# Weight sums formed in place in the raw tiles of a hybrid-attention encoder layer, five raw blocks read instead of eight

## The chip, the cores and the metric

The kernel runs on one core of a Trainium2 chip. The metric is the device time of one execution in microseconds (us). A core has TensorE (PE, with its weight loads PEld), VectorE (DVE), ScalarE (ACT), GpSimd (POOL) and SyncE (SP); SP issues nearly all transfers here, each engine works through its own instructions in order, and engines wait for each other through semaphores.

## The reference

One encoder layer on 512 tokens of width 2048, in float32:

```python
h = rmsnorm(x, g_mix); proj = einsum('bsd,de->bse', h, w_in)      # 2048 -> 4608
out_a = rmsnorm(mixer_a(qa, ka, va, ...)); out_b = rmsnorm(mixer_b(qb, kb, vb))
x = x + einsum('bse,ed->bsd', concat([out_a, out_b]), w_out)
h2 = rmsnorm(x, g_ffn)
gate, up = split(einsum('bsd,df->bsf', h2, w_gate_up), 2)         # 2048 -> 2 x 5632
x = x + einsum('bsf,fd->bsd', silu(gate) * up, w_down)            # 5632 -> 2048
return rmsnorm(x, g_final)
```

## The kernel before, in words

The program has four stages in time: the input projection with the attention heads worked in between (0 to about 620 us), the output projection (`out_chunk`, kinds A and B, to about 732 us), eleven gate/up blocks (`gate_up_block`, to about 1630 us) and six down blocks (`down_block`, to about 2045 us), then a last plain piece of the down projection (`last_down`, `finish`).

Every float32 product is made of three PE matmuls in a reduced float32 type: each operand is split into a high part (an ACT copy) and a low part (a DVE subtraction), and `mm3` multiplies high by high, high by low and low by high. A 128x512 matmul takes one slot of the PE.

A gate/up or down block (`ColBlock`) is one two-by-two matrix product by seven products instead of eight (the forms m1, m7, m6, m2, m5, m4, m3, in this order, `CHAIN`). The activations' sums lie in the two `arena` tiles. The weights of a block come in quarters; for a batch g (there are four in a gate/up block and in the first four down blocks, two in the last two) the quarters are raw blocks of 128x1024, 512 KB each. Call them a = (0,0), b = (0,1), c = (1,1), d = (1,0). The seven forms need a; c-b; c-b+a; d; b-a; d-(c-b+a); c. One form of one batch is one unit (`Cols`): its weight operand is split into a "twin" tile tw (`split_hi` on ACT, L703; `split_lo` on DVE, L706), three twins exist (`TWINS`), and its matmuls are 12: two column pieces, two row tiles, three products. 28 units make a block of four batches.

Before the change each form loads its own raw blocks (tag raw, six buffers) and each sum is written to a tile of its own (tag sum, L732). a, b and c are loaded twice by this and, with d and m7's second operand, a batch reads eight blocks.

The order of the work is set by the program: for unit n, `prepare(n)` first issues loads (`load_raws`) as far as a look-ahead in time and the number of buffers allow, then makes the high part of a unit about 7 us ahead (`COLS_AHEAD`, two to three units), and the low part of the unit before that one; then come the matmuls of unit n, hooks (`box.after`) and one entry of the queue `side`. `load_raws` loads nothing further when the buffers are all held by blocks whose last unit has not had its low part made. Hooks of a gate/up block do the work on its results: `snap` copies a form's result out of PSUM, `low` and `high` multiply gate by up, `turn(k)` transposes 128 columns on the PE, `pair_sums` forms the sums of two turned pieces for the down blocks on DVE, and `store` writes them to DRAM. `h_side` does the same for the output projection's result: four transposes and an ACT copy for each half of a pair, then sums on DVE, a high part on ACT and a low part on DVE into `arena`. `ready` holds back the first block's matmuls on a pair until its `h_side` was issued.

Of the kernel before, what the change touches and what calls it, by code (L numbers as in the profile page):

```python
# [62 lines left out]
def encoder_block(ctx, tc, x, g_mix, w_in, g_q_a, g_k_a, g_out_a, g_out_b, w_out, g_ffn,  # L63
# [112 lines left out]

    def split(src, name, gain=None, between=None, at=None, tag=None):
        if at is None:
            hi, lo = (slot(name + "h", F32R), slot(name + "l", F32R)) if tag is None else (wslot(tag), wslot(tag))
# [23 lines left out]
    class Raw:  # L203
        def __init__(self, pieces, first=0):
            self.pieces, self.first, self.t = pieces, first, None

        def load(self):
            if self.t is None:
                self.t = wp.tile([P, 2 * 512], F32, tag="raw", bufs=RAWS, name=nm("raw"))
                for src, dst in self.pieces(self.t):  # L210
                    if self.first:
                        for a in range(src.shape[1]):
                            nc.sync.dma_start(dst[:, a], src[:, a])
                            load_x(self.first + a)
                    else:
                        nc.sync.dma_start(dst, src)
# [361 lines left out]
    def out_chunk(kind, c):  # L578
        box = {}
        base = 0 if kind == "A" else NHA  # L580

        def early(k):
            if (kind, k) not in oS:
                drain_until(lambda: (kind, k) in oT)
                oS[kind, k] = split(oT.pop((kind, k)), "oS", go[:, base + k:base + k + 1],
                                    at=42 + 2 * k if k < 7 else None, tag="wi")

# [12 lines left out]

        def mm(u, k):
            if k == 0:
                box["ps"] = [bank("pw") for _ in range(NT)]
# [4 lines left out]
            for t in range(NT):  # L608
                mm3(box["ps"][t], cols(oS[kind, k], t * P), u.w, k == 0, k == NHA - 1)

        def post():
# [9 lines left out]
            if kind == "B":  # L621
# [7 lines left out]
        add_chunk(w_out, [(base + k) * P for k in range(NHA)], [(c * 512, 0, 512)], mm, post,  # L629
                  early if kind == "B" else None,  # L630
# [9 lines left out]
    def pair_sums(w):  # L640
# [9 lines left out]
        tt(s4, b_l, s2)  # L650
        return w[:, 256:].rearrange("p (f c) -> p f c", c=256)

# [7 lines left out]
    def h_side(i, half):  # L660
        k = 2 * i + half
        c, j = divmod(k, 4)
        ps = bank("x1t")
        for n, t in enumerate((2, 3, 0, 1) if half == 0 else range(NT)):
            nc.tensor.transpose(ps[:, n * P:(n + 1) * P], x1[c][t][:, j * P:(j + 1) * P], ident)
        if half == 0:
            hpart[0] = sp.tile([P, 4 * 512], F32, tag="pair", bufs=1, name=nm("pair"))
        nc.scalar.activation(hpart[0][:, half * 512:(half + 1) * 512], ps, AF.Copy, scale=gf[:, k:k + 1])
# [23 lines left out]
    class Cols(Unit):  # L692
        ahead = COLS_AHEAD
        dur = COLS_US

# [4 lines left out]
        def split_hi(self):  # L700
            self.src = self.box.weights(self.form, self.g, *[r.t for r in self.raws])
            self.pair = sp.tile([P, 2, 2 * 512], F32R, tag="twin", bufs=TWINS, name=nm("tw"))
            nc.scalar.activation(self.pair[:, 0], self.src, AF.Copy)  # L703

        def split_lo(self):
            nc.vector.tensor_tensor(self.pair[:, 1], self.src, f32(self.pair[:, 0]), op=OP.subtract)  # L706

        def mm(self, u):
            self.box.multiply(self)

    class ColBlock:
        def __init__(self, w, row, lo, pairs, ready=None):
            self.pairs, self.ready = pairs, ready
            self.ps, self.sums = {}, {}
            self.begin = len(units)
            batches = pairs // 2

            def raw(i, j, g):
                def pieces(t):
                    rows = w[0, row + 4 * g * P:row + 4 * (g + 1) * P, lo[j]:lo[j] + 512]  # L720
                    return [(rows.rearrange("(q i p) c -> i p q c", q=2, i=2)[i],
                             t.rearrange("p (q c) -> p q c", q=2))]
                return Raw(pieces)
            need = {"m1": ((0, 0),), "m7": ((1, 1), (0, 1)), "m6": ((0, 0),), "m2": ((1, 0),),
                    "m5": ((0, 1), (0, 0)), "m4": (), "m3": ((1, 1),)}
            for form in CHAIN:
                for g in range(batches):
                    units.append(Cols(self, form, g, [raw(i, j, g) for i, j in need[form]]))

        def weights(self, form, g, *t):  # L730
            def tt(d, a, b, op=OP.subtract):
                nc.vector.tensor_tensor(d, a, b, op=op)  # L732
                return d

            def new():
                return sp.tile([P, 2 * 512], F32, tag="sum", bufs=SUMS, name=nm("sum"))
            if form == "m7":
                self.sums[g] = tt(new(), *t)
                return self.sums[g]
            if form == "m6":  # L740
                return tt(self.sums[g], self.sums[g], t[0], OP.add)
            if form == "m2":
                tt(self.sums[g], t[0], self.sums[g])
            if form == "m5":
                return tt(new(), *t)
            if form == "m4":
                return self.sums.pop(g)
            return t[0]

# [16 lines left out]
        def after(self, form, late, f):  # L766
            hook(self.begin + (CHAIN.index(form) + 1) * (self.pairs // 2) - 1 + late, f)

    def gate_up_block(f0):
# [50 lines left out]
        def store(n):  # L820
            nc.sync.dma_start(forms_dram[:, :, n], pair_sums(st["pair"]))

# [176 lines left out]
    def load_raws(n):  # L999
        while done["load"] < len(units) and at[done["load"]] <= at[n] + units[done["load"]].load_ahead:  # L1000
            for raw in units[done["load"]].raws:
                if raw.t is None:
                    live[:] = [r for r in live if last_use[r] >= done["lo"]]
                    if len(live) == RAWS:
                        return
# [108 lines left out]
```

## Time and profile before

| | |
|---|---|
| three runs | 2106.68, 2109.05, 2121.43 us; median 2109.05 |
| the profiled execution | 2104.86 us, span 2103.0 us, clock 0.99 |
| busy share of the span | PE 97%, PEld 79%, DVE 67%, ACT 47%, POOL 6% |
| moved | 419.78 MB, 200 GB/s in the mean |
| loads of gate/up weights | 352 of 512 KB |
| loads of down weights | 168 of 512 KB |
| chain that ended last | PE 72%, DMA 12%, DVE 10%, issue 3%, ACT 2% |

A row of a group gives line, engine, operation, output<-input and count, then busy time and the mean of one in ns, then the idle time of the engine just before these instructions and what ended it. A row of waits gives engine and instruction, what it waited for, total, times and longest in us.

### The profile page before, as it was taken

What the parts mean: (1) busy time and instruction counts of PE and PEld (TensorE: products, weight loads), DVE (VectorE), ACT (ScalarE), POOL (GpSimd) and SP (SyncE); (2) the same over time, 40 slices, a digit from 0 to 9 for tenths busy, and PEclk for the clock granted to TensorE, in tenths of its full rate; (3) what the DMA queues carried; (4) which work ended last, traced back from release to release, by engine and by line L of the source; (5) the groups of instructions that cost most, each with busy time, mean ns of one, the idle gap of its engine ahead of it and who ended that gap; (6) DMA issues with size and microseconds to landing.
All of it is one profiled execution on the core that took longest, in us unless ns stands there. A gap on an engine that the chain in (4) does not pass through costs nothing.

```text
span 2103.0 us, 24686 instructions
## 1 busy us (share of the span) xinstructions
PE 2037.1 (97%) x9159; PEld 1663.0 (79%) x9159; DVE 1418.2 (67%) x1862; ACT 985.5 (47%) x1406; POOL 129.6 (6%) x135
## 2 busy tenths in 40 slices
PE   9999999999999989999999999999999999999997
PEld 7888888888887768788888788888777777887876
DVE  5565655555645577777787777877778758757666
ACT  5333344444443544444444444444445455545663
POOL 3100100000000000000000000000000111111220
PEclk9999999999999999999999999999999999999999
DMA  7322222223343366677676676776778899999994
GB/s 232 104 80 81 86 71 81 81 76 106 120 166 122 101 213 215 226 252 230 228 253 228 220 242 225 243 236 232 242 240 278 262 264 328 295 247 327 266 316 172
DMA packets 238201, 419.78 MB, mean 200 GB/s; under 512 B 14800, under 2 KB 57856, under 8 KB 238080
## 3 DMA queue, kind: packets, MB, share of 16 engines
q1 hardware_dynamic: 224080, 392.96, 56.1%
q0 software_dynamic: 11808, 21.50, 6.0%
q10 hardware_dynamic: 2192, 3.74, 0.5%
q8 instruction: 71, 1.16, 0.2%
q14 instruction: 50, 0.41, 0.1%
HBM read 365.19 MB, written 52.95 MB: 199 GB/s over the span
## 4 chain that ended last, share of the span: by engine, by line
PE 72%; DMA 12%; DVE 10%; issue 3%; ACT 2%; SPq 1%; ACTq 0%; DVEq 0%; POOLq 0%
PE zc L195 8%; PE zc L196 7%; PE zc L194 7%; PE pj L194 6%; PE pj L196 6%; PE pj L195 6%; DMA raw<-in_w_down_dram 5%; DMA raw<-in_w_gate_up_dram 5%; PE yc L195 5%; PE yc L196 5%; PE yc L194 5%; DVE tw L706 4%; DVE sum L732 4%; PE pw L195 2%; PE pw L196 2%
## 5 line engine op out<-in xcount | busy, mean ns | idle before, releaser
L195 PE MATMUL zc<-tw,arena 128*128 128x512 f32 x1024 | 405.7, 396 | 28.8 <-DVE tw L706 28.7
L703 ACT ACTIVATE tw<-sum 128x1024 fp32r<-128x1024 f32 x256 | 269.5, 1061 | 323.0 <-DVE sum L732 205.3
L194 PE MATMUL zc<-tw,arena 128*128 128x512 f32 x1024 | 404.9, 395 | 3.5 <-ACT arena L672 2.8
L196 PE MATMUL zc<-tw,arena 128*128 128x512 f32 x1024 | 403.2, 394 | 1.3 <-DVE arena L673 1.3
L706 DVE TENSOR_TENSOR tw<-sum,tw 128x1024 fp32r<-128x1024 f32 x256 | 311.6, 1221 | 81.3 <-ACT tw L703 79.9
L706 DVE TENSOR_TENSOR tw<-raw,tw 128x1024 fp32r<-128x1024 f32 x192 | 234.7, 1223 | 125.5 <-ACT tw L703 123.8
L703 ACT ACTIVATE tw<-raw 128x1024 fp32r<-128x1024 f32 x192 | 203.1, 1059 | 205.5 <-PE zc L196 115.3
L195 PEld LDWEIGHTS zc<-tw,arena 128*128 128x128 f32 x1024 | 194.7, 190 | 78.7 <-DVE tw L706 39.0
L194 PE MATMUL pj<-w,arena 128*128 128x512 f32 x576 | 229.3, 398 | 1.2 <-ACT w L232 1.2
L194 PEld LDWEIGHTS zc<-tw,arena 128*128 128x128 f32 x1024 | 194.4, 190 | 44.4 <-ACT arena L672 3.2
L196 PEld LDWEIGHTS zc<-tw,arena 128*128 128x128 f32 x1024 | 194.9, 190 | 42.1 <-DVE arena L673 1.8
L195 PE MATMUL pj<-w,arena 128*128 128x512 f32 x576 | 225.3, 391 | 0.9 <-DVE w L237 0.9
L196 PE MATMUL pj<-w,arena 128*128 128x512 f32 x576 | 225.7, 392 | 0.0
L732 DVE TENSOR_TENSOR sum<-raw,raw 128x1024 f32<-128x1024 f32 x128 | 156.6, 1223 | 90.3 <-DMA raw<-in_w_down_dram 46.1
L195 PE MATMUL yc<-tw,arena 128*128 128x512 f32 x512 | 202.0, 395 | 10.7 <-DVE tw L706 10.7
L194 PE MATMUL yc<-tw,arena 128*128 128x512 f32 x512 | 202.9, 396 | 0.0
L196 PE MATMUL yc<-tw,arena 128*128 128x512 f32 x512 | 200.9, 392 | 0.0
L237 DVE TENSOR_TENSOR w<-raw,w 128x512 fp32r<-128x512 f32 x192 | 140.6, 747 | 27.2 <-ACT w L232 15.9
L890 POOL DMA_DIRECT2D x1d<-ev x82 | 72.4, 959 | 1238.7 <-ACT ev L889 1205.8
L232 ACT ACTIVATE w<-raw 128x512 fp32r<-128x512 f32 x192 | 115.1, 626 | 49.0 <-PE pj L196 25.9
L196 PEld LDWEIGHTS pj<-w,arena 128*128 128x128 f32 x576 | 108.5, 188 | 24.2 <-DVE arena L189 0.5
L195 PEld LDWEIGHTS pj<-w,arena 128*128 128x128 f32 x576 | 108.7, 189 | 23.5 <-DVE w L237 1.2
(201 smaller groups left out, 2995.6 us busy)
## 6 DMA issues: line engine op xcount, KB each, us to landing
raw<-in_w_gate_up_dram SPq DMA_DIRECT2D x352, 512.0 KB, 4.9
raw<-in_w_down_dram SPq DMA_DIRECT2D x168, 512.0 KB, 7.6
x1d<-ev POOLq DMA_DIRECT2D x82, 256.0 KB, 6.9
raw<-in_w_in_dram SPq DMA_DIRECT2D x38, 512.0 KB, 3.7
forms<-pair SPq DMA_DIRECT2D x20, 896.0 KB, 5.1
fr<-forms SPq DMA_DIRECT2D x35, 512.0 KB, 5.1
raw<-in_w_in_dram SPq DMA_DIRECT2D x68, 256.0 KB, 3.0
raw<-in_w_out_dram SPq DMA_DIRECT2D x32, 512.0 KB, 4.9
```

The costliest lines, as they stand in the source:

```text
L194: nc.tensor.matmul(dst, ah, bh, start=start, stop=False, skip_group_check=chained)
L195: nc.tensor.matmul(dst, ah, bl, start=False, stop=False, skip_group_check=chained)
L196: nc.tensor.matmul(dst, al, bh, start=False, stop=stop, skip_group_check=chained)
L232: nc.scalar.activation(self.w[0], src, AF.Copy)
L237: nc.vector.tensor_tensor(self.w[1], self.src, f32(self.w[0]), op=OP.subtract)
L703: nc.scalar.activation(self.pair[:, 0], self.src, AF.Copy)
L706: nc.vector.tensor_tensor(self.pair[:, 1], self.src, f32(self.pair[:, 0]), op=OP.subtract)
L732: nc.vector.tensor_tensor(d, a, b, op=op)
L890: nc.gpsimd.dma_start(x1_dram[2 * cb + j, row], e, accum_op=OP.add)
```

## The change

The raw blocks of a batch get a pool of their own (tag craw, ten buffers) and stay there; the sums are written over them. `fold`, a new function, runs right after the low part of the units m1 and m2. A batch now loads a and b (for m1), c (for m7), d (for m2), and c again as e (for m3). Loads for these units look 14 us ahead (`COLS_LOAD`) instead of 24 us. In the first block the unit m1 of batch 3 stands behind m7 of batches 0 and 1. `h_side` and the work on gate/up results are cut into more steps, with the store three units after the sums. The last chunk of the output projection takes its heads in the order 6, 7, 0 to 5, and its weight tiles are 12 instead of 10.

```diff
+COLS_LOAD = 14.0
-RAWS = 6
-SUMS = 6
-W_TILES = {"wi": 12, "wo": 10, "wl": 32}
+RAWS = {"raw": 6, "craw": 10}
+W_TILES = {"wi": 12, "wo": 12, "wl": 32}
...
+        order = [6, 7, 0, 1, 2, 3, 4, 5] if (kind, c) == ("B", NC - 1) else list(range(NHA))
...
                     side.append(lambda i=i: h_side(i, 1))
+                    side.append(lambda i=i: h_side(i, 2))
...
         if half == 1:
-            src = pair_sums(hpart.pop(0))
+            pair_sums(hpart[0])
+        if half == 2:
+            src = hpart.pop(0)[:, 256:].rearrange("p (f c) -> p f c", c=256)
             hi, lo = (arena[i // 4][:, :, i % 4, j] for j in range(2))
...
     class Cols(Unit):
         ahead = COLS_AHEAD
+        load_ahead = COLS_LOAD
...
         def split_lo(self):
             nc.vector.tensor_tensor(self.pair[:, 1], self.src, f32(self.pair[:, 0]), op=OP.subtract)
+            self.box.fold(self.form, self.g)
...
-            need = {"m1": ((0, 0),), "m7": ((1, 1), (0, 1)), "m6": ((0, 0),), "m2": ((1, 0),),
-                    "m5": ((0, 1), (0, 0)), "m4": (), "m3": ((1, 1),)}
+                return Raw(pieces, tag="craw")
+            self.raws = [{n: raw(i, j, g) for n, i, j in (("a", 0, 0), ("b", 0, 1), ("c", 1, 1), ("d", 1, 0),
+                                                          ("e", 1, 1))} for g in range(batches)]
+            need = {"m1": "ab", "m7": "cb", "m6": "ca", "m2": "dc", "m5": "a", "m4": "c", "m3": "e"}
+            order = [(form, g) for form in CHAIN for g in range(batches)]
+            if ready is not None:
+                order.insert(5, order.pop(3))
...
+        def weights(self, form, g):
+            t = {n: r.t for n, r in self.raws[g].items()}
             if form == "m7":
+                nc.vector.tensor_tensor(t["b"], t["c"], t["b"], op=OP.subtract)
             if form == "m6":
+                nc.vector.tensor_tensor(t["c"], t["c"], t["a"], op=OP.subtract)
+            return t[{"m1": "a", "m7": "b", "m6": "c", "m2": "d", "m5": "a", "m4": "c", "m3": "e"}[form]]
+
+        def fold(self, form, g):
+            t = {n: r.t for n, r in self.raws[g].items()}
+            if form == "m1":
+                nc.vector.tensor_tensor(t["a"], t["b"], t["a"], op=OP.subtract)
             if form == "m2":
+                nc.vector.tensor_tensor(t["c"], t["d"], t["c"], op=OP.subtract)
...
         for k in range(4):
-            box.after("m3", 4 + 2 * k, lambda k=k: turn(k))
+            late = (3, 4, 10, 11)[k]
+            box.after("m3", late, lambda k=k: turn(k))
             if k % 2 and f0 + k < F_PLAIN:
-                box.after("m3", 5 + 2 * k, lambda k=k: store((f0 + k) // 2))
+                box.after("m3", late + 1, lambda: pair_sums(st["pair"]))
+                box.after("m3", late + 4, lambda k=k: store((f0 + k) // 2))
```

How the instructions move is shown at two places, both at the form m7 of the fourth gate/up block. The first place is DVE. Before, where L706 is a low part, L732 a sum, L803 the product `high`:

```order
L706 TENSOR_TENSOR tw_8077<-raw_8003,tw_8077 128x1024 [waits DMAHW7_49,Activation_49]
L803 TENSOR_TENSOR s_1459_7692<-s_1459_7692,s_1469_7778 128x1024
L732 TENSOR_TENSOR sum_8116<-raw_8041,raw_8058 128x1024 [waits DMAHW2_49,DMAHW1_49]
L706 TENSOR_TENSOR tw_8098<-raw_8022,tw_8098 128x1024 [waits DMAHW0_49,Activation_49]
L732 TENSOR_TENSOR sum_8135<-raw_8075,raw_8096 128x1024 [waits DMAHW4_49,DMAHW3_49]
L706 TENSOR_TENSOR tw_8118<-sum_8116,tw_8118 128x1024 [waits Activation_49]
L732 TENSOR_TENSOR sum_8166<-raw_8114,raw_8133 128x1024 [waits DMAHW6_49,DMAHW5_49]
L706 TENSOR_TENSOR tw_8137<-sum_8135,tw_8137 128x1024 [waits Activation_49]
L732 TENSOR_TENSOR sum_8189<-raw_8162,raw_8164 128x1024 [waits DMAHW7_49,DMAHW0_49]
L706 TENSOR_TENSOR tw_8168<-sum_8166,tw_8168 128x1024 [waits PE_49,Activation_49]
```

DVE with the change, where L712 is a low part, L751 the fold of m1, L743 the sum of m7, L808 `high`, L649 the pair sums; raw_7888, 7907, 7928 and 7949 are b of batches 0 to 3, and raw_7966, 7984, 8072 and 8096 are c of batches 0 to 3:

```order
L712 TENSOR_TENSOR tw_7986<-raw_7926,tw_7986 128x1024 [waits DMAHW5_49,Activation_49]
L751 TENSOR_TENSOR raw_7926<-raw_7928,raw_7926 128x1024 [waits DMAHW6_49,DVE_49]
L808 TENSOR_TENSOR s_1406_7609<-s_1406_7609,s_1415_7694 128x1024
L743 TENSOR_TENSOR raw_7888<-raw_7966,raw_7888 128x1024 [waits DMAHW1_49]
L712 TENSOR_TENSOR tw_8006<-raw_7947,tw_8006 128x1024 [waits DMAHW7_49,Activation_49]
L751 TENSOR_TENSOR raw_7947<-raw_7949,raw_7947 128x1024 [waits DMAHW0_49,DVE_49]
L743 TENSOR_TENSOR raw_7907<-raw_7984,raw_7907 128x1024 [waits DMAHW2_49]
L712 TENSOR_TENSOR tw_8024<-raw_7888,tw_8024 128x1024 [waits Activation_49]
L743 TENSOR_TENSOR raw_7928<-raw_8072,raw_7928 128x1024 [waits DMAHW3_49]
L712 TENSOR_TENSOR tw_8048<-raw_7907,tw_8048 128x1024 [waits PE_49,Activation_49]
```

```order
L649 TENSOR_TENSOR pair_8045<-pair_8045 128x256 [waits DVE_49] x2
L743 TENSOR_TENSOR raw_7949<-raw_8096,raw_7949 128x1024 [waits DMAHW4_49]
L712 TENSOR_TENSOR tw_8075<-raw_7928,tw_8075 128x1024 [waits PE_49,Activation_49]
L745 TENSOR_TENSOR raw_7966<-raw_7966,raw_7886 128x1024
L712 TENSOR_TENSOR tw_8099<-raw_7949,tw_8099 128x1024 [waits Activation_49]
```

The second fence goes on where the first ends, less three rows of the pair sums. A fold now stands behind each low part of m1, and the sum of m7's batch 2, which waits for the transfer of c into raw_8072, stands right behind the low part that reads raw_7888 and ahead of the low part of batch 1.

The second place is SP, at the loads for the same units. Before:

```order
L216 DMA raw_8075<-in_w_gate_up_dram 128x2x512 [waits DMAHW5_49,DVE_49]
L216 DMA raw_8096<-in_w_gate_up_dram 128x2x512 [waits DMAHW6_49,DVE_49]
L216 DMA raw_8114<-in_w_gate_up_dram 128x2x512 [waits DMAHW7_49,DVE_49]
L216 DMA raw_8133<-in_w_gate_up_dram 128x2x512 [waits DMAHW1_49,DVE_49]
L216 DMA raw_8162<-in_w_gate_up_dram 128x2x512 [waits DMAHW2_49]
```

SP with the change:

```order
L216 DMA raw_7966<-in_w_gate_up_dram 128x2x512 [waits DMAHW1_49,DVE_49]
L216 DMA raw_7984<-in_w_gate_up_dram 128x2x512 [waits DMAHW2_49,DVE_49]
L216 DMA raw_8072<-in_w_gate_up_dram 128x2x512 [waits DMAHW3_49,DVE_49]
L216 DMA raw_8096<-in_w_gate_up_dram 128x2x512 [waits DMAHW4_49,DVE_49]
L216 DMA raw_8130<-in_w_gate_up_dram 128x2x512 [waits DMAHW6_49,DMAHW5_49,DVE_49]
L826 DMA forms<-pair_8045 896x1x256
```

The load into raw_8072 takes the buffer of raw_7888: with a and b of four batches and c of two, all ten buffers are held until the low part of m7's batch 0 (tw_8024) has read b of batch 0. The load into raw_8096 takes raw_7907's buffer in the same way, behind tw_8048. The store of the pair sums has no semaphore of DVE to wait for any more.

More of the change, by code (lines that the diff above doesn't have):

```diff
@@ L175, in rsqrt_mean, with split @@
         return r
-    def split(src, name, gain=None, between=None, at=None, tag=None):
+    def split(src, name, gain=None, between=None, at=None):
         if at is None:
-            hi, lo = (slot(name + "h", F32R), slot(name + "l", F32R)) if tag is None else (wslot(tag), wslot(tag))
+            hi, lo = slot(name + "h", F32R), slot(name + "l", F32R)
         else:
@@ L627, in post @@
                     side.append(lambda i=i: h_side(i, 1))
+                    side.append(lambda i=i: h_side(i, 2))
                 side.append(lambda: park_x1(c))
-        add_chunk(w_out, [(base + k) * P for k in range(NHA)], [(c * 512, 0, 512)], mm, post,
+        add_chunk(w_out, [(base + k) * P for k in order], [(c * 512, 0, 512)], mm, post,
                   early if kind == "B" else None,
@@ L660, in h_side @@
     def h_side(i, half):
[L661 to L668, printed above, removed]
+        if half < 2:
+            k = 2 * i + half
+            c, j = divmod(k, 4)
+            ps = bank("x1t")
+            for n, t in enumerate((2, 3, 0, 1) if half == 0 else range(NT)):
+                nc.tensor.transpose(ps[:, n * P:(n + 1) * P], x1[c][t][:, j * P:(j + 1) * P], ident)
+            if half == 0:
+                hpart[0] = sp.tile([P, 4 * 512], F32, tag="pair", bufs=1, name=nm("pair"))
+            nc.scalar.activation(hpart[0][:, half * 512:(half + 1) * 512], ps, AF.Copy, scale=gf[:, k:k + 1])
         if half == 1:
-            src = pair_sums(hpart.pop(0))
+            pair_sums(hpart[0])
+        if half == 2:
+            src = hpart.pop(0)[:, 256:].rearrange("p (f c) -> p f c", c=256)
             hi, lo = (arena[i // 4][:, :, i % 4, j] for j in range(2))
@@ L700, in split_hi @@
         def split_hi(self):
-            self.src = self.box.weights(self.form, self.g, *[r.t for r in self.raws])
+            self.src = self.box.weights(self.form, self.g)
             self.pair = sp.tile([P, 2, 2 * 512], F32R, tag="twin", bufs=TWINS, name=nm("tw"))
@@ L713, in __init__ @@
             self.pairs, self.ready = pairs, ready
-            self.ps, self.sums = {}, {}
-            self.begin = len(units)
+            self.ps, self.at = {}, {}
             batches = pairs // 2
@@ L722, in pieces @@
                              t.rearrange("p (q c) -> p q c", q=2))]
-                return Raw(pieces)
-            need = {"m1": ((0, 0),), "m7": ((1, 1), (0, 1)), "m6": ((0, 0),), "m2": ((1, 0),),
-                    "m5": ((0, 1), (0, 0)), "m4": (), "m3": ((1, 1),)}
[L726 to L736, printed above, removed]
+                return Raw(pieces, tag="craw")
@@ new lines, in __init__ @@
+            self.raws = [{n: raw(i, j, g) for n, i, j in (("a", 0, 0), ("b", 0, 1), ("c", 1, 1), ("d", 1, 0),
[4 more added lines that the diff above has]
+                order.insert(5, order.pop(3))
+            for form, g in order:
+                self.at[form] = len(units)
+                units.append(Cols(self, form, g, [self.raws[g][n] for n in need[form]]))
@@ L766, in after @@
         def after(self, form, late, f):
-            hook(self.begin + (CHAIN.index(form) + 1) * (self.pairs // 2) - 1 + late, f)
+            hook(self.at[form] + late, f)
     def gate_up_block(f0):
```

29 lines of the change are left out of this document (10 added, 19 removed).

## The prediction, made before the changed kernel ran

> **What bounds the kernel now.** I read the page's busy line first, then the waits of PE, then stretches of time, then one block's DVE rows.
>
> ```profile
> PE 2037.1 (97%) x9159; PEld 1663.0 (79%) x9159; DVE 1418.2 (67%) x1862; ACT 985.5 (47%) x1406; POOL 129.6 (6%) x135
> ...
> PE zc L195 <- DVE tw L706: 28.7, 22, 3.9
> PE yc L195 <- DVE tw L706: 10.7, 8, 4.0
> PE pw L195 <- DVE w L237: 5.3, 6, 1.6
> ```
>
> PE is the bound, and when it waits, it waits for DVE's low parts. So an edit counts only through what it does to these waits. How much is there to win? The stretches (columns: us, busy time and count of PE, PEld, DVE, ACT, POOL, then granted clock, DMA share, GB/s), two moments at which ACT copies m6 out of PSUM (in the first and the eleventh gate/up block), the first plain product after the down blocks, and two PE rows twelve matmuls apart with one group of four transposes:
>
> ```profile
> 660.00:760.00 100.00, 86.15 (x376) 67.64 (x375) 60.94 (x85) 49.12 (x75) 1.86 (x1) 0.95 0.40 128
> 779.00:1585.00 806.00, 792.17 (x3525) 648.27 (x3524) 608.86 (x614) 373.68 (x425) 0.00 (x0) 0.99 0.71 234
> 1585.00:2040.00 455.00, 433.57 (x1874) 352.03 (x1874) 322.18 (x280) 247.14 (x276) 70.62 (x80) 0.99 0.96 287
> ...
> 779.28 1.28 ACT L781 ACTIVATE s<-zc 128x512 f32<-128x512 f32 x2 [0.97 <-PE zc L196]
> 1584.58 1.28 ACT L781 ACTIVATE s<-zc 128x512 f32<-128x512 f32 x2 [1.34 <-PE zc L196]
> ...
> 2045.37 0.39 PE L194 MATMUL fd<-w,acth 128*128 128x512 f32 x1
> ...
> 1104.43 0.39 PE L195 MATMUL xc<-tw,arena 128*128 128x512 f32 x1
> 1107.15 0.39 PE L195 MATMUL zc<-tw,arena 128*128 128x512 f32 x1
> ...
> 834.33 0.44 PE at L810 x4
> ```
>
> A unit at full speed takes 1107.15 - 1104.43 = 2.72 us, so a gate/up block needs 28 x 2.72 + 4 x 0.44 = 77.9 us. From m6 of block 1 to m6 of block 11 are ten blocks: 1584.58 - 779.28 = 805.3 us against 779. About **26 us** are lost there in all, 2.6 a block. From there to the plain product are 16 + 140 units, 426 us with the transposes, and 460.8 pass: **35 us** lost. In the 100 us around the change from output projection to gate/up PE is idle for 13.9, and the clock of 0.95 costs some 5: **19 us**.
>
> One block's start on DVE (L706 low part, L732 sum, L800 `low`, L803 `high`):
>
> ```profile
> 1059.83 1.23 DVE L706 TENSOR_TENSOR tw<-raw,tw 128x1024 fp32r<-128x1024 f32 x1 [1.45 <-ACT tw L703]
> 1060.97 1.28 DVE L800 TENSOR_TENSOR s<-zc,s 128x512 f32<-128x512 f32 x2
> 1062.55 1.23 DVE L706 TENSOR_TENSOR tw<-raw,tw 128x1024 fp32r<-128x1024 f32 x1 [0.30 <-ACT tw L703]
> 1063.69 1.22 DVE L803 TENSOR_TENSOR s<-s,s 128x1024 f32<-128x1024 f32 x1
> 1064.82 1.22 DVE L732 TENSOR_TENSOR sum<-raw,raw 128x1024 f32<-128x1024 f32 x1
> 1065.96 1.22 DVE L706 TENSOR_TENSOR tw<-raw,tw 128x1024 fp32r<-128x1024 f32 x1
> 1067.09 1.22 DVE L732 TENSOR_TENSOR sum<-raw,raw 128x1024 f32<-128x1024 f32 x1
> 1068.31 1.22 DVE L706 TENSOR_TENSOR tw<-sum,tw 128x1024 fp32r<-128x1024 f32 x1
> 1070.42 1.23 DVE L732 TENSOR_TENSOR sum<-raw,raw 128x1024 f32<-128x1024 f32 x1 [0.89 <-DMA raw<-in_w_gate_up_dram]
> 1071.57 1.22 DVE L706 TENSOR_TENSOR tw<-sum,tw 128x1024 fp32r<-128x1024 f32 x1
> 1073.78 1.22 DVE L732 TENSOR_TENSOR sum<-raw,raw 128x1024 f32<-128x1024 f32 x1 [0.99 <-DMA raw<-in_w_gate_up_dram]
> ```
>
> Three things are to be seen: back to back such an instruction costs 1.135 us (1064.82 to 1065.96); `low` begins when the block before has ended, so the block starts near 1060.8, call it T; and a late transfer stops DVE for about 1 us only, because each load is issued three or more DVE instructions ahead of its use.
>
> **The change, part by part.** *Transfers.* A batch reads five blocks instead of eight, so 520 loads of 512 KB become 325. DVE's work does not fall: four sums a batch before, four now (m7, m6 and the two folds). PE's and ACT's work is the same. So nothing is won but waits.
>
> *The new wait.* The order on DVE puts the sum of m7's batch 2 right behind the low part that frees the buffer its transfer needs. SP cannot issue that load earlier, DVE has nothing else to do until it lands, and the low part of m7's batch 1, for which PE waits next, is queued behind. Batch 3 repeats it, with only the pair sums (1.56 us in the trace) for cover. Its price comes from these rows (two windows, and the raw tiles from 1050 to 1080 us):
>
> ```profile
> raw<-in_w_gate_up_dram SPq DMA_DIRECT2D x4, 512.0 KB, 3.6
> raw<-in_w_gate_up_dram SPq DMA_DIRECT2D x9, 512.0 KB, 6.0
> L216 SPq DMA_DIRECT2D raw<-in_w_gate_up_dram x13: 367/368/462, 1050.2 to 1075.0; - x13
> L703 ACT ACTIVATE tw<-raw x6: 1061/1062/1062, 1050.6 to 1064.2; 128x1024 fp32r<-128x1024 f32 x6
> DMA to landing us min/median/max: 3.5/3.9/7.6
> ```
>
> With few loads in flight (1115 to 1135 us) a block lands in 3.6 us, among many (1060 to 1080) in 6.0. At the new place hardly another load is in flight, so I take 3.6, plus 0.37 of issue and an estimated 0.1 for signals: 4.1. Then:
>
> - From `low` to the low part of m7's batch 0 DVE has `low` (1.28) and eight instructions of 1.135, 10.4 us, pushed back by up to 1.1 by the fold ahead of `low`: done at T + 10.6 to 11.7.
> - PE starts m7's batch 0 at T + 4 x 2.72 + 2 x 0.44 = T + 11.8, just served. It wants the low part of batch 1 one unit and one matmul later, T + 14.7.
> - That low part comes after 4.1 + 1.2 (sum) + 1.2: T + 17.1 to 18.2. PE stands for 2.4 to 3.5 us.
> - The low part of batch 2 comes another 6.5 later, T + 23.6 to 24.7, and would have been wanted at T + 17.4. So the block is 6.2 to 7.3 us late, **7 taken**.
> - After that DVE needs 2.27 a unit against PE's 2.72 and gets ahead again. The late loads of d (m2, batches 2 and 3) have about two to four us of DVE work between buffer and use and come just in time by the same count, since PE has two transposes there: nothing.
>
> Bounds for this: below, DVE could be as far ahead as the three twins allow. The twin for m7's batch 0 comes free when m1's batch 1 ends, T + 5.4, then 1.06 on ACT and 1.23 on DVE: T + 7.9. Then the second wait ends at T + 21 and the block is 3.6 late. Above, with 6.0 to land, both waits grow by 2.4, to 12.
>
> Ten blocks (2 to 11) have this: 10 x 7 = 70, and the 26 lost there now goes, because each other load has ten or more us of DVE work ahead of it. **+44 us** (bounds +10 and +94).
>
> *Down blocks.* Here DVE has no `low`, `high` or pair sums, so the low part of m7's batch 0 ends near T + 9.5, but transfers share the queues with accumulations, at a DMA share of 0.96 before. I take 5.0 to land. Blocks one and three have both waits, as on the gate/up side: 9.5 + 2 x (5.5 + 2.4) = 25.3 against 16.5, 9 late each; blocks two and four have one, with copies of the sums into `arena` between: about 6 each (estimate, between one wait's 3.6 and 9); the last two, of two batches, fit in ten buffers, 4 together. That is 34 against 35: **0** (bounds -25, if the lighter traffic frees the stage, and +20, at the stage's old landing:
>
> ```profile
> raw<-in_w_down_dram SPq DMA_DIRECT2D x166, 512.0 KB, 7.6
> SPq L821 <- DVE pair L646: 115.8, 20, 6.5
> ```
>
> first row). The second row is what SP waited at the store of the pair sums. That wait goes, but the loads behind it are held by their buffers now, so I give it nothing; were they not, it would be worth up to 6 us of SP's time a store.
>
> *Start of gate/up.* `h_side` in three steps keeps DVE from standing behind ACT's copy into `arena`, and the moved m1 gives the last pairs two units more. Of the 19 us I take **-12** (bounds 0 and -19). The new order of the last chunk and two more weight tiles belong to this.
>
> *Sum.* The profiled execution took 2104.9: 2104.9 + 44 + 0 - 12 = 2136.9. The median of the runs is 4.2 above it, so the forecast on that scale is **2141 us**.
>
> A rule to weigh: PE's clock. The row that bears on it is a wait of PE in the eleventh block, from the chain of waits:
>
> ```profile
> 1511.90 1.23 DVE sum L732
> 1513.13 1.15 DVE tw L706
> 1514.32 0.67 PE zc L195
> 1514.99 0.43 PE zc L196
> ...
> 1518.23 0.23 PE zc L195
> ```
>
> After it matmuls come at 0.43 instead of 0.23 us for about nine of them, 1.8 us. In my sum this is free: slower matmuls after the first wait only shorten the second, which ends on DVE. The Trainium skill, "TensorE: Matmul & The Clock Gate", Part 1, says the clock halves after an idle window of about 3.4 us that runs freely, so a gap near that length sometimes escapes. My first gap lies at that length.
>
> **The rivals.**
>
> 1. *Half clock after the second wait, or slower landing.* If the first gap leaves the clock alone, the second is 6.5 - 2.5 = 4 us long and 1.8 follow, ten times: 2159. With landing at 6.0: 2141 + 50 = 2191. For it: the row of 6.0. Against: a lone load.
> 2. *DVE is far enough ahead.* The lower bound of 3.6 a block: 2141 - 34 = 2107, no change. For it: in the rows above DVE still waits for ACT at the start of the block. Against: from there to m7 it is busy without a gap, with three folds more.
> 3. *Faster: the traffic was the price.* The down stage runs at a share of 0.96, and a batch now needs five blocks of eight. If lighter queues clear the stage (-25), the start gives all its 19, and the lower bound holds: 2109 + 10 - 25 - 19 = 2075. It decides from the point where landing in the down stage falls below about 4 us. Against it: two waits a block that no traffic makes.
> 4. *It does not act.* The order shows it does; 2109 if some other wait ends last in each block.
>
> **How the numbers follow.** A measurement of this kernel can tell about 1%, 21 us. Forecast 0.48, rival 1 0.20, rival 2 0.16, rival 3 0.13, rival 4 0.03. Slower by over 1% (above 2130): rival 1 and most of the forecast, 0.63. Within 1%: rivals 2 and 4 and the lower edge of the forecast, 0.23. Faster by over 1%: 0.14. The forecast's own range is 2120 to 2165; the range of eight in ten reaches from 2086, which leaves out most of rival 3, to 2188.
>
> **What would show it.** Right: in each of blocks 2 to 11 the sum of m7 waits for the transfer of gate/up weights twice, about 4 and 2.5 us; PE waits for DVE tw twice a block, 65 to 75 us in all; a block lasts about 85 us; the DMA share falls from 0.71 to about 0.45 in gate/up; the stretch at 660 to 760 is about 12 us shorter. Wrong: blocks of 80 us or less, or DVE that waits there without PE waiting; or a down stage that changes by more than 20 us.

## The result and the profile after

The changed kernel takes 2179.21 us (median; 2177.59 to 2183.56) against 2107.97 us for the kernel before on the same chip: a ratio of 1.0326, interval 1.0281 to 1.0371. Slower was forecast, with gate/up as the place; the size was not, nor any loss in the down stage: 32 us forecast, 71 measured. The profiled execution took 2180.45 us with a span of 2178.3, 75.3 us more span than before.

The busy line of the changed kernel:

```profile
PE 2061.0 (95%) x9159; PEld 1676.4 (77%) x9159; DVE 1420.7 (65%) x1862; ACT 989.8 (45%) x1406; POOL 129.9 (6%) x135
```

DVE's work is what it was (1418.2 before). Its waits and PE's (L712 is now the low part, L743 the sum of m7; total, times, longest in us):

```profile
PE yc L195 <- DVE tw L712: 72.9, 30, 5.4
DVE raw L743 <- DMA raw<-in_w_gate_up_dram: 61.5, 20, 3.8
DVE raw L743 <- DMA raw<-in_w_down_dram: 27.4, 6, 6.1
PE zc L195 <- DVE tw L712: 9.7, 8, 1.8
```

and, of the first of these rows, the part in the ten blocks from 772 to 1636 us:

```profile
PE yc L195 <- DVE tw L712: 51.4, 20, 3.9
```

PE's wait at yc, the bank of m7 (and of m4), was 10.7 us in the whole kernel before, only 0.4 of it in these ten blocks. Now it is 72.9, and 51.4 of it stand here. DVE's twenty waits in gate/up are two in each of ten blocks. The stretches, with the columns of those before:

```profile
660.00:760.00 100.00, 88.98 (x408) 70.45 (x407) 70.28 (x93) 51.41 (x77) 1.86 (x1) 1.00 0.38 128
772.00:1636.00 864.00, 811.83 (x3521) 659.78 (x3520) 610.61 (x615) 378.58 (x425) 0.00 (x0) 0.97 0.48 146
1636.00:2119.00 483.00, 444.26 (x1890) 357.75 (x1889) 324.80 (x284) 251.03 (x286) 72.36 (x82) 0.98 0.77 206
```

ACT's copy of m6 in blocks 1 and 11 and the first plain product, in the order of time:

```profile
771.73 1.28 ACT L786 ACTIVATE s<-zc 128x512 f32<-128x512 f32 x2 [0.98 <-PE zc L196]
1635.87 1.28 ACT L786 ACTIVATE s<-zc 128x512 f32<-128x512 f32 x2 [0.54 <-PE zc L196]
2119.28 0.39 PE L194 MATMUL fd<-w,acth 128*128 128x512 f32 x1
```

So m6 of block 1 comes 7.5 us earlier, the ten blocks from there take 864.1 us instead of 805.3 (**+58.8**), the down stage 483.4 instead of 460.8 (**+22.6**), the tail 1.4 more. The DMA share in gate/up fell from 0.71 to 0.48 and the time rose.

The first part of m7 in one block on DVE (L649 pair sums):

```profile
1087.05 1.22 DVE L712 TENSOR_TENSOR tw<-raw,tw 128x1024 fp32r<-128x1024 f32 x1
1091.95 1.23 DVE L743 TENSOR_TENSOR raw<-raw,raw 128x1024 f32<-128x1024 f32 x1 [3.69 <-DMA raw<-in_w_gate_up_dram]
1093.10 1.22 DVE L712 TENSOR_TENSOR tw<-raw,tw 128x1024 fp32r<-128x1024 f32 x1
1094.23 1.54 DVE L649 TENSOR_TENSOR pair<-pair 128x256 f32<-128x256 f32 x4
1098.19 1.22 DVE L743 TENSOR_TENSOR raw<-raw,raw 128x1024 f32<-128x1024 f32 x1 [2.42 <-DMA raw<-in_w_gate_up_dram]
1099.34 1.22 DVE L712 TENSOR_TENSOR tw<-raw,tw 128x1024 fp32r<-128x1024 f32 x1
```

The low part ends, its buffer is free, DVE stands 3.7 us for the transfer into it, makes the sum and only then the low part that PE wants; then once more, with the pair sums as cover. And PE in two later blocks (each row a matmul, L195 the one that reads the low part; in the brackets PE's idle time):

```profile
1176.40 0.39 PE L194 MATMUL yc<-tw,arena 128*128 128x512 f32 x1
1179.63 0.50 PE L195 MATMUL yc<-tw,arena 128*128 128x512 f32 x1 [2.85 <-DVE tw L712]
...
1182.30 0.39 PE L194 MATMUL yc<-tw,arena 128*128 128x512 f32 x1
1185.74 0.79 PE L195 MATMUL yc<-tw,arena 128*128 128x512 f32 x1 [3.05 <-DVE tw L712]
1186.33 0.63 PE L196 MATMUL yc<-tw,arena 128*128 128x512 f32 x1
1186.76 0.63 PE L194 MATMUL yc<-tw,arena 128*128 128x512 f32 x1
...
1441.02 0.79 PE L195 MATMUL yc<-tw,arena 128*128 128x512 f32 x1 [2.69 <-DVE tw L712]
1441.61 0.63 PE L196 MATMUL yc<-tw,arena 128*128 128x512 f32 x1
...
1445.06 0.40 PE L194 MATMUL yc<-tw,arena 128*128 128x512 f32 x1
1447.05 0.50 PE L195 MATMUL yc<-tw,arena 128*128 128x512 f32 x1 [1.59 <-DVE tw L712]
```

In the first of them the matmuls behind the second gap come 0.43 us apart (1186.33 to 1186.76) instead of 0.23: half clock. In the second the half clock lies between the two gaps, and the second gap is so much shorter. Such blocks differ in length by 3 us (from m6 to m6; granted clock in the third column from the right):

```profile
1291.26:1378.99 87.73, 81.84 (x353) 66.47 (x352) 60.80 (x62) 37.49 (x43) 0.00 (x0) 0.96 0.46 141
1378.99:1463.78 84.79, 80.44 (x353) 65.47 (x352) 60.63 (x62) 37.50 (x43) 0.00 (x0) 0.98 0.48 146
```

### The profile page after: what moved, and what is told of

Same layout as the page of the kernel before. It is cut to its first block, busy times and chain, and to the rows that moved or that the text cites. A ratio compares the mean times of both kernels' runs of the same rounds, so it can differ in the third digit from the quotient of the medians.

```text
span 2178.3 us, 24416 instructions
## 1 busy us (share of the span) xinstructions
PE 2061.0 (95%) x9159; PEld 1676.4 (77%) x9159; DVE 1420.7 (65%) x1862; ACT 989.8 (45%) x1406; POOL 129.9 (6%) x135
## 4 chain that ended last, share of the span: by engine, by line
PE 38%; DVE 10%; DMA 9%; issue 6%; ACT 2%; POOL 1%; SPq 0%; ACTq 0%; POOLq 0%; DVEq 0%
PE zc L196 6%; PE zc L194 6%; PE zc L195 6%; DVE tw L712 5%; DMA raw<-in_w_gate_up_dram 4%; PE yc L195 4%; PE yc L196 4%; PE yc L194 4%; DMA raw<-in_w_down_dram 3%; DVE raw L743 2%; PE xc L195 2%; ACT tw L709 1%; PE xc L196 1%; PE xc L194 1%; POOL x1d L897 1%
## 5 line engine op out<-in xcount | busy, mean ns | idle before, releaser
L709 ACT ACTIVATE tw<-raw 128x1024 fp32r<-128x1024 f32 x448 | 471.3, 1059 | 599.7 <-PE zc L196 181.0
L712 DVE TENSOR_TENSOR tw<-raw,tw 128x1024 fp32r<-128x1024 f32 x448 | 545.3, 1222 | 293.6 <-ACT tw L709 283.0
L195 PE MATMUL zc<-tw,arena 128*128 128x512 f32 x1024 | 400.5, 391 | 9.7 <-DVE tw L712 9.7
L195 PE MATMUL yc<-tw,arena 128*128 128x512 f32 x512 | 214.6, 419 | 72.9 <-DVE tw L712 72.9
L195 PEld LDWEIGHTS zc<-tw,arena 128*128 128x128 f32 x1024 | 192.9, 188 | 51.6 <-DVE tw L712 12.6
L195 PE MATMUL pj<-w,arena 128*128 128x512 f32 x576 | 225.1, 391 | 0.9 <-DVE w L237 0.9
L194 PE MATMUL yc<-tw,arena 128*128 128x512 f32 x512 | 211.3, 413 | 0.6 <-ACT tw L709 0.6
L196 PE MATMUL yc<-tw,arena 128*128 128x512 f32 x512 | 210.6, 411 | 0.0
L195 PEld LDWEIGHTS yc<-tw,arena 128*128 128x128 f32 x512 | 102.8, 201 | 108.0 <-DVE tw L712 86.6
L743 DVE TENSOR_TENSOR raw<-raw,raw 128x1024 f32<-128x1024 f32 x64 | 78.1, 1221 | 89.0 <-DMA raw<-in_w_gate_up_dram 61.5
L196 PEld LDWEIGHTS pj<-w,arena 128*128 128x128 f32 x576 | 108.4, 188 | 23.7
L195 PEld LDWEIGHTS pj<-w,arena 128*128 128x128 f32 x576 | 108.6, 189 | 23.4 <-DVE w L237 1.2
L194 PEld LDWEIGHTS pj<-w,arena 128*128 128x128 f32 x576 | 108.5, 188 | 23.4 <-ACT w L232 1.1
```

The source lines that it names most:

```text
L194: nc.tensor.matmul(dst, ah, bh, start=start, stop=False, skip_group_check=chained)
L195: nc.tensor.matmul(dst, ah, bl, start=False, stop=False, skip_group_check=chained)
L196: nc.tensor.matmul(dst, al, bh, start=False, stop=stop, skip_group_check=chained)
L743: nc.vector.tensor_tensor(t["b"], t["c"], t["b"], op=OP.subtract)
```

## The experiments

All times by stage, each from one profiled execution (m6 of block 1; the ten blocks from there to m6 of block 11; from there to the first plain product), with the median of the runs and the ratio to the kernel before:

| kernel | m6 at | ten blocks | down | median | ratio, interval |
|---|---|---|---|---|---|
| before | 779.3 | 805.3 | 460.8 | 2107.97 | |
| after | 771.7 | 864.1 | 483.4 | 2179.21 | 1.0326, 1.0281 to 1.0371 |
| e1 two c | 772.1 | 785.6 | 450.6 | 2068.32 | 0.9810, 0.9781 to 0.9840 |
| e2 low parts first | 780.0 | 856.7 | 506.0 | 2200.19 | 1.0437, 1.0403 to 1.0472 |
| e3 swap everywhere | 772.2 | 820.0 | 477.1 | 2129.90 | 1.0099, 1.0067 to 1.0130 |
| e4 forms on POOL | 772.7 | 861.2 | 489.6 | 2185.05 | 1.0364, 1.0326 to 1.0402 |
| e5 one wait | 769.8 | 825.9 | 470.5 | 2129.19 | 1.0110, 1.0067 to 1.0154 |
| e6 weave | 771.8 | 785.5 | 469.9 | 2086.64 | 0.9894, 0.9857 to 0.9930 |
| e7 old turns, stores | 770.4 | 872.6 | 496.7 | 2203.17 | 1.0462, 1.0423 to 1.0500 |
| e8 start alone | 770.7 | 804.6 | 468.0 | 2101.66 | 0.9969, 0.9947 to 0.9992 |
| e9 weave, forms on POOL | 769.9 | 785.1 | 477.1 | 2093.45 | 0.9921, 0.9899 to 0.9942 |
| e10 two c, forms on POOL | 774.6 | 785.7 | 447.2 | 2067.91 | 0.9798, 0.9777 to 0.9818 |
| e11 weave before | 769.1 | 807.7 | 465.1 | 2100.10 | 0.9948, 0.9929 to 0.9968 |
| e12 weave, two d | 771.5 | 784.7 | 457.8 | 2073.16 | 0.9825, 0.9798 to 0.9852 |

**e1: is the transfer of c the price?**

```diff
+            for g in range(2, batches):
+                self.raws[g]["c"] = self.raws[g - 2]["c"]
             need = {"m1": "ab", "m7": "cb", ...
```

> Leaves out: batches 2 and 3 of a gate/up or down block take their c from the tiles of batches 0 and 1, so two of the 20 loads of a four-batch block are not made (m7, m6, m2 and m4 of these batches multiply wrong weights); every instruction on PE, DVE and ACT stays. Theory (the late transfer of c in m7 is the price): DVE no longer waits at the sum of m7, a gate/up block falls from 86.4 to about 78.5 us, ten blocks give back 75 to 80, the four large down blocks another 10 to 20: about 2085 us (2070 to 2100). Rival (DVE's own work, four sums and folds in new places, is what is late): PE goes on waiting for DVE tw about 80 us and the time stays within 15 us of 2179.

Its busy line, and from the order of time ACT's copies of m6 in blocks 1 and 11 (the code stands two lines lower in this kernel):

```profile
PE 2023.3 (98%) x9159; PEld 1658.2 (80%) x9159; DVE 1420.9 (69%) x1862; ACT 988.4 (48%) x1406; POOL 129.9 (6%) x135
```

```profile
772.11 1.28 ACT L788 ACTIVATE s<-zc 128x512 f32<-128x512 f32 x2 [0.98 <-PE zc L196]
1557.71 1.28 ACT L788 ACTIVATE s<-zc 128x512 f32<-128x512 f32 x2 [0.54 <-PE zc L196]
```

DVE has the same 1862 instructions and 1421 us, yet a block lasts 78.56 us instead of 86.41: all of the loss in gate/up goes with the two loads of c. The down stage gave more than expected, 32.8 us. What e1 can't tell is whether the two loads' traffic or their lateness counts; for gate/up, e6 does.

**e2: only the order of two DVE instructions.**

```diff
             load_raws(n)
+            if isinstance(units[done["hi"]], Cols):
+                while done["lo"] < done["hi"]:
+                    units[done["lo"]].split_lo()
+                    done["lo"] += 1
             units[done["hi"]].split_hi()
```

> Nothing is left out. In column blocks every low part that is pending is made ahead of the next sum, so the low part of m7's batch 1 stands ahead of the sum that waits for the transfer. Theory (the price is what is queued behind the waiting sum, not the wait itself): the transfer of batch 2 gets 2.3 us of DVE work as cover and that of batch 3 gets 3.7; PE's first wait in a block goes, the second shrinks to 1 to 3 us; a gate/up block falls from 86.4 to 79.5 to 82; the kernel to about 2125 us (2105 to 2145). Rival (each block waits for a transfer anyway, whatever stands behind): DVE's waits only move, 2165 to 2185.

Wrong by 75 us. The long gaps went (PE's wait at yc fell to 32.0 us), but a block still lasts 85.7. DVE in m7 and m6 of a block (L745 the sum of m6):

```profile
1103.74 1.23 DVE L712 TENSOR_TENSOR tw<-raw,tw 128x1024 fp32r<-128x1024 f32 x1 [1.26 <-ACT tw L709]
1104.89 1.22 DVE L745 TENSOR_TENSOR raw<-raw,raw 128x1024 f32<-128x1024 f32 x1
1107.37 1.22 DVE L712 TENSOR_TENSOR tw<-raw,tw 128x1024 fp32r<-128x1024 f32 x1 [1.26 <-ACT tw L709]
1108.52 1.22 DVE L745 TENSOR_TENSOR raw<-raw,raw 128x1024 f32<-128x1024 f32 x1
1110.99 1.23 DVE L712 TENSOR_TENSOR tw<-raw,tw 128x1024 fp32r<-128x1024 f32 x1 [1.26 <-ACT tw L709]
```

A unit now takes 1107.37 - 1103.74 = 3.63 us: sum on DVE, high part on ACT, low part on DVE, one behind the other, where PE needs 2.72. The kernel's old order, sum of the next unit ahead of the low part of this one, is what hides ACT's 1.06 us. I had costed the edit by what it frees and not by what it puts in series.

**e3: more room from the order of the units.**

```diff
-            if ready is not None:
+            if batches == 4:
                 order.insert(5, order.pop(3))
```

> Nothing is left out. What the change does in the first gate/up block (m1 of batch 3 behind m7 of batches 0 and 1) is done in every block of four batches, down blocks too. The buffer for c of batch 2 is then freed one unit earlier on DVE, and PE has one more unit that waits for no transfer. Theory: by the order the low part of m7's batch 1 stands ahead of the waiting sum, m1 of batch 3 and m7 of batch 2 come about as PE wants them, 0 to 2 us lost a block: about 2110 us (2095 to 2130). Rival (buffers are short anyway; the wait moves to the next load of the block): a block stays above 84 us and the time within 15 us of 2179.

The cause held, the size not quite: 82.0 us a block, where 78 to 80 were meant, and the median is at the upper edge. DVE's wait in m7 came once a block (26.3 us in ten waits) and PE still stood for it.

**e5: one wait instead of two.**

```diff
+            for g in range(3, batches):
+                self.raws[g]["c"] = self.raws[g - 2]["c"]
```

> Leaves out: only batch 3 of a four-batch block takes its c from the tile of batch 1 (one of 20 loads is not made; m7, m6, m2 and m4 of that batch multiply wrong weights). The first of the two waits stays, with the low part of m7's batch 1 behind it; the second is gone. By the working of the prediction PE then stands once, about 3 us, and a gate/up block lasts 78.4 + 3 = 81.4 us; with about 15 us from the down stage the kernel takes about 2115 us (2105 to 2125). If a gap of 3 us halves PE's clock behind it, which is the rival, blocks last 83 to 84 us and the kernel 2130 to 2140. If DVE stays behind for the rest of the block after one wait, blocks stay near 86 and the time near 2170.

DVE's remaining wait in one block (L745 the sum of m7 in this kernel), and the stretch of that block:

```profile
1160.58 1.22 DVE L745 TENSOR_TENSOR raw<-raw,raw 128x1024 f32<-128x1024 f32 x1 [3.60 <-DMA raw<-in_w_gate_up_dram]
```

```profile
1101.40:1183.44 82.04, 78.69 (x353) 64.49 (x352) 60.70 (x62) 37.50 (x42) 0.00 (x0) 1.00 0.48 145
```

From block 5 to block 10 every block lasts 82.0 to 82.1 us, with no half clock behind a gap as long as the first one of the changed kernel. In blocks 2, 3, 4 and 11 the same gap, 2.7 to 3.0 us, was followed by matmuls at half clock, and they last 82.6 to 84.0 us. Block 3, its stretch and the matmuls behind its gap:

```profile
853.79:936.70 82.91, 79.96 (x353) 65.72 (x352) 60.76 (x62) 37.50 (x42) 0.00 (x0) 0.98 0.47 143
...
915.69 0.50 PE L195 MATMUL yc<-tw,arena 128*128 128x512 f32 x1 [2.95 <-DVE tw L712]
...
916.30 0.63 PE L194 MATMUL yc<-tw,arena 128*128 128x512 f32 x1
916.73 0.63 PE L195 MATMUL yc<-tw,arena 128*128 128x512 f32 x1
```

So one wait costs 3.6 us where the clock is spared, and the second adds 4.4 in the mean, part of it half clock. The rival of this run, half clock behind a single gap, held in four blocks of ten, and the median lies 4 us above the band given.

**e6: the same ten buffers and loads in an order that frees them earlier.**

```diff
-            if ready is not None:
-                order.insert(5, order.pop(3))
+            if batches == 4:
+                order[:8] = [order[k] for k in (0, 1, 4, 2, 5, 3, 6, 7)]
```

> Nothing is left out. In every block of four batches the units of m1 and m7 are woven: m1 of batches 0 and 1, m7 of 0, m1 of 2, m7 of 1, m1 of 3, m7 of 2 and 3. Each m7 then frees the buffer of its b while m1 still has units to run, and by the order 5 us or more of DVE work stand between the free buffer and the sum that waits for its transfer, against 0 and 1.5 in the changed kernel. Theory (a transfer of 4.1 us behind 0 and 1.5 us of cover is the whole price): gate/up comes to 78.4 to 79.5 us a block as without the loads, the down stage to 450 to 465 us, the kernel to about 2080 us (2068 to 2095), under both kernels. Rival (ten buffers are too few in any order, the wait goes to d of m2, whose loads have 3.7 and 2.3 us of cover, or to e): blocks above 82 us, 2120 or more.

Its loads of gate/up weights on the page (count, KB, us to landing), and its two stretches:

```profile
raw<-in_w_gate_up_dram SPq DMA_DIRECT2D x220, 512.0 KB, 4.3
```

```profile
772.00:1557.00 785.00, 784.33 (x3520) 644.29 (x3519) 607.06 (x612) 375.99 (x424) 0.00 (x0) 1.00 0.52 160
1557.00:2027.00 470.00, 444.04 (x1892) 358.00 (x1891) 325.50 (x287) 248.73 (x286) 72.28 (x82) 0.98 0.79 212
```

All 220 loads are made, PE is busy for 784.33 of 785 us at full clock, and the ten blocks take what they take in e1: not the traffic, the lateness was the price. This version beats both kernels, the one before by about 1%: 2086.64 us, 0.9894 of its time. Only the down stage, meant for 450 to 465 us, takes 469.9.

**e7: the old places of turns, sums and stores.**

```diff
-            late = (3, 4, 10, 11)[k]
+            late = 4 + 2 * k
...
-                box.after("m3", late + 4, lambda k=k: store((f0 + k) // 2))
+                box.after("m3", late + 1, lambda k=k: store((f0 + k) // 2))
```

> Nothing is left out. The turns, the pair sums and the stores of a gate/up block stand again where they stood before the change (turns 4, 6, 8, 10 units behind m3, sums and store right behind each pair). The pair sums no longer stand between the two waits, so DVE's second wait grows from 2.5 to about 4.1 us and the sums follow later; SyncE waits for the sums at the store, ahead of a load of d. Theory (the late sums and stores are worth nothing while loads are held by their buffers): within 10 us of 2179. Rival (the later store is what keeps SyncE free): 10 us or more slower, with SyncE waiting at the store for DVE.

The rival: 24 us slower than the changed kernel, with SP at the store again (SP's waits):

```profile
SPq L826 <- DVE pair L649: 192.6, 20, 11.2
```

In gate/up it is 8.5 us, 6.3 of them in the last block; DVE's waits for c grew from 61.5 to 76.0 us there, and PE waits 7.8 us at zc and 5.3 at xc, where the changed kernel has 0.7 at both together. In the down stage it is 13.3 us, and why is not settled: only its first block has such hooks. The edit moves the turns and the pair sums too, so it prices all of them together.

**e4, e9, e10: who issues the forms.** In the down stage SP stands at L874 for accumulations, 60.1 us in eight waits, with raw blocks queued behind. The edit alone (e4), with the weave (e9) and with e1 (e10):

```diff
-                nc.sync.dma_start(st["t"], forms_dram[:, m, first + 4 * h:first + 4 * h + 4])
+                nc.gpsimd.dma_start(st["t"], forms_dram[:, m, first + 4 * h:first + 4 * h + 4])
```

> Nothing is left out. In the down stage the loads of the pair forms (fr) are issued by GpSimd instead of SyncE, so SyncE does not stand in front of a form whose buffer waits for an accumulation while raw loads queue behind it. Theory (part of the 22.6 us that the down stage lost comes from SyncE blocked at L874, 60 us in eight waits): the down stage is 8 to 20 us shorter, about 2165 us (2157 to 2173), gate/up unchanged. Rival (all of the down stage's loss is the wait of m7 for its own buffers, SyncE's waits lie beside it): within 5 us of 2179.

> Nothing is left out. The woven order of e6, and the loads of the pair forms issued by GpSimd as in e4. Theory (moving the forms gave nothing in e4 because the waits of m7 ended later in the same blocks; with those gone, SyncE standing at the forms, 54 us in seven waits, sets when raw blocks land in the down stage): the down stage falls from 469.9 to 456 to 464 us, the kernel from 2087 to about 2079 us (2074 to 2083). Rival (the down stage's rest is transfers that land in 6 us behind 2 to 4.5 us of cover, whoever issues the forms): within 4 us of 2087.

> Leaves out the same two loads of c a block as e1; the loads of the pair forms are issued by GpSimd. Here no wait of m7 is left, and 24.6 us are still lost in the down stage, the largest piece where SyncE stood at a form and m1 of the third block came late. Theory: 8 to 14 us of them go, the down stage lasts 437 to 443 us, the kernel 2055 to 2061 us. Rival (SyncE's stand is not what these blocks wait for): within 4 us of 2068.

The theory failed three times: 5.8 us slower than the changed kernel, 6.8 slower than e6, equal to e1. A stand at the forms moved with the loads to POOL, where the accumulations are issued behind them. Whether that made e4 and e9 slower is not shown. POOL's row of waits in e9's down stage:

```profile
POOL fr L874 <- DVE arena L880: 23.3, 5, 6.3
```

A long wait of a queue, then, was no measure of what it costs.

**e8 and e11: the parts without the sums.** e8 is the kernel before with the way into gate/up of the changed one (chunk order, weight tiles, `h_side` in three steps, the first block's swap); e11 puts the woven order into it as well, in place of the first block's swap:

```diff
-            for form in CHAIN:
-                for g in range(batches):
...
+            order = [(form, g) for form in CHAIN for g in range(batches)]
+            if batches == 4:
+                order[:8] = [order[k] for k in (0, 1, 4, 2, 5, 3, 6, 7)]
```

> Nothing is left out. The kernel before with only the parts of the change that touch the way into gate/up: the order of the last output chunk, the split into the arena instead of weight tiles, two more weight tiles, h_side in three steps, m1 of batch 3 of the first block behind two m7 units. Sums, buffers and loads of column blocks are those of before. Theory: m6 of the first block comes about 7.5 us earlier, as in the changed kernel, and nothing else moves: 2099 us (2093 to 2104). Rival (the start is paced by the loads of gate/up weights, eight a batch): no gain, 2104 to 2110.

> Nothing is left out. The kernel of e8 (the old sums, six raw tiles, eight loads a batch) with the woven order of e6 in every four-batch block. Theory (the gain of e6 over the kernel before comes from five loads a batch and ten buffers once their cover is there, not from the order as such): within 10 us of e8, 2092 to 2112, gate/up not under 800 us. Rival (the order alone keeps PE fed): gate/up 790 or less, 2088 or less.

Both as the theory had it: m6 comes 8.6 us earlier in e8, its ten blocks take 804.6 us, and the order alone brings nothing to them (807.7). Only with five loads a batch and ten buffers does it pay. The down stage of e8, in which no instruction was edited, is 7.2 us longer than before; differences of that size between single traces can't be told there.

**e12: d in the down stage.**

```diff
+            for g in range(2, batches) if w is w_down else ():
+                self.raws[g]["d"] = self.raws[g - 2]["d"]
```

> Leaves out: the woven kernel e6, with batches 2 and 3 of a four-batch down block taking their d from the tiles of batches 0 and 1 (two of 20 loads of these blocks are not made; m2 and the sums of c behind it multiply wrong weights). Gate/up is that of e6. Theory (what the woven kernel still loses in the down stage against e1, 469.9 to 450.6 us, is the late d, whose loads land in about 6 us behind 2.3 us of cover there): the waits of PE at xc, about 8 us with the clock behind them, go, the down stage lasts 456 to 463 us, the kernel 2074 to 2080 us. If it is m1 and m7 (zc and yc, 14 us of gaps), it stays within 4 us of 2087.

The down stage falls from 469.9 to 457.8 us. PE's waits at xc, the bank of m2, which needs d, fall there from 8.4 us in e6 to 2.2, and those at zc and yc together stay at 17.6 us. So where a block lands in 6.1 us, the loads of d cost about 12 us with the clock behind the waits. Two loads a block are not made here, and the run can't tell their lateness from their traffic.

## Why the prediction was right or wrong, point by point

- **The new wait: right.** Two waits of DVE a block were forecast at about 4 and 2.5 us: 3.69 and 2.42 in the block shown. PE's waits were to be 65 to 75 us in these blocks and are 51.4; the 72.9 at yc counts the down stage too. Lateness of a block 6.2 to 7.3 us: the gaps and the half clock between them, which DVE's low part ends, come to 64 us in ten blocks, 6.4 each. So the forecast of the lateness held, and a part of it is slow matmuls instead of waits. e1 and e6 show that nothing else was the price in gate/up, so rivals 2, 3 and 4 fall: the traffic did fall to 0.48 and brought nothing while these waits stood. With the waits gone (e6) the ten blocks are 20 us shorter than before; whether lighter traffic or more buffers made that, no run separates.
- **+44 at gate/up was +58.8: the term is mis-sized, in two places.** The first step that failed is "in my sum this is free". Half clock came behind the second gap in six of ten blocks, about 2.1 us each, 12.6 in all, on top of the lateness. I had reasoned that slow matmuls only shorten the next gap; that holds where they lie between the gaps (the block at 1441), not behind the second. And "the 26 lost there now goes" was too much by 6.6: without any wait (e1) a block takes 78.56, not 77.9. Together: 64.3 + 12.6 + 6.6 - 26.3 = 57.2 of the 58.8.
- **0 at the down stage was +22.6, the larger miss and more than the 20 us that the prediction named as a sign of being wrong: the failed step is "34 against 35".** The 34 of new waits is near the 32.8 that e1 takes away. But the 35 lost before did not go: 24.6 stay (450.6 against 426) when no c is late. In e1's trace PE waits 15.2 us there, 12.9 of it at zc, for low parts of DVE and high parts and copies of ACT. What makes these late stays open; none of the runs took them away, and the prediction let the 35 go without naming a cause. The term for d ("nothing") held in gate/up, where e6's blocks take 78.4 us with all loads of d made; for the down stage the prediction gave d no term, and in the woven order the loads of d cost some 12 us there (e12).
- **-12 at the start was -7.5**, and e8 alone gives -8.6: inside its bounds.
- **The late stores, "I give it nothing": not borne out.** Put back, turns, sums and stores cost 24 us (e7), in a kernel that still has the two waits. How much of this is the stores, and how much would be left without the waits, no run shows.

The clock, beside the rule that the prediction weighed: the Trainium skill, "TensorE: Matmul & The Clock Gate", Part 1, has the half clock follow an idle window of about 3.4 us that runs freely. The traces differ: gaps well below that length are followed by it too, and not each time (2.85 us was not, 2.69 was). In the changed kernel it followed the first gap (2.7 to 2.9 us) in six blocks of ten and the second (1.4 to 3.9 us) in six; no block was without it. Behind the single gap of e5 it came in four blocks of ten, and in none of the six that have a gap of 2.6 to 2.7 us every 82.0 to 82.1 us. By the Trainium skill's window of 3.413 us, 82.04 us are 24.04 windows, so each of those gaps would meet the window at nearly the same place; this is an estimate that no run here tests.

## What to carry to other kernels

When loads are made fewer by keeping tiles longer, count for each load the work that stands between the instruction that frees its buffer and the one that needs it, on the engine that waits; here 0 and 1.5 us stood against a transfer of about 4, and weaving two products so that 5 us stand there turned +71 us into -22. Look at what an order already hides (e2) before swapping two instructions of it. And don't take old losses off a sum without naming what makes them.

## What the runs showed of the hardware

- The landing of a 512 KB block hangs on the stage: medians of 4.3 to 4.4 us in gate/up and 6.1 to 6.3 in the down stage, in the changed kernel, e1 and e6 alike, at DMA shares of about 0.5 and 0.8. With 108 loads of down weights in place of 168 it fell from 7.6 to 6.3 only (the page of the changed kernel):

```profile
raw<-in_w_gate_up_dram SPq DMA_DIRECT2D x220, 512.0 KB, 4.4
raw<-in_w_down_dram SPq DMA_DIRECT2D x108, 512.0 KB, 6.3
```

- Half clock follows idle gaps of PE of 2.6 to 3.0 us at times and at other times not. Over a block of gate/up the granted clock was 0.96 to 0.98 with two such gaps, and with one gap (e5) 0.96 to 0.98 in four blocks and 1.00 in those where it did not set in.
